# Sixteen transfers within HBM, given out behind the attention's gated products instead of at set planner times

## The chip, the cores and the metric

The kernel runs on one core of one Trainium2 chip. The metric is the device time of one execution in microseconds, as the median of several runs. Engine names in the profile: PE is TensorE (matmuls; PEld its weight loads), DVE is VectorE, ACT is ScalarE, POOL is GpSimd, SP is SyncE, which here only issues DMAs.

## The reference

One decoder block over 512 tokens of width 1024, in fp32:

```python
h = rms_norm(x, norm_pre)
proj = h @ w_in                       # q_n, six k/v of the attention, gates, z_n, q_r, k_r, v_r, z_r, m_a, m_b
o_a = nsa(...)                        # compressed, selected and sliding branch, gated and summed, per head
y_a = (o_a * silu(z_n)) @ w_nsa_o
o_b = retention(...)                  # four heads, chunks of 128, a running state, group norm
y_b = (o_b * silu(z_r)) @ w_ret_o
merged = sigmoid(m_a) * y_a + sigmoid(m_b) * y_b
y = x + rms_norm(merged @ w_out, norm_post)
```

The product `o_a * silu(z_n)` is what is called the gated product here.

## The kernel before

Every fp32 matrix product is made of three matmuls of rounded parts: high times high, high times low, low times high. The weights lie in one stream in HBM, in the order of use, in blocks of 128 rows by 1024 columns (512 KB). SyncE loads a block into one of four `raw` buffers (`NR`, line 28); a splitter then rounds each half to its high part `whi` (ScalarE or VectorE) and takes the rest `wlo` (VectorE, line 209). The next load into that buffer goes out when both halves are split (`load_next`, lines 347 to 369).

The order of work by products: the six keys and values, the gates, the queries, two hidden products of the compressed keys and values, and then `PLAN` (line 30): the gate Z, the merge gate MA of the first half, the retention's ZR, QK and VR twice over, with MB, NO and RO, and the second half. The attention's heads are worked between these products, token tile 3 first and 0 last. The last products are those with `w_out`.

Two of the products of the plan, the second halves of MA and MB (`SEVEN`, line 32), are done in Strassen's manner: seven products of half blocks instead of eight. This needs sums of quarter blocks of the weights. They are made in HBM, by DMAs that GpSimd issues, before the loads of those products read them as `raw<-t`. Per product there are four scratch tensors `t1` to `t4` (512 KB each) and eight transfers: four copies (t1 = b11, t3 = b12, t2 = b11, t4 = b21) and four that accumulate (t1 += b12, t3 += b22, t2 += t3, t4 += t2). With two products that makes 16, which go in turn for the one and the other (`weight_sums`, lines 327 to 337). An accumulation onto t2 needs the sums in t3, and one onto t4 needs t2.

The instructions are given out by a planner, `Order` (lines 45 to 118): each piece of work is a generator, which yields a planner time (or a condition, or a time with an engine) before it gives out instructions. The planner takes the pieces in the order of rank and of readiness, and keeps a clock per engine from fixed costs. The order in which it gives out an engine's instructions is the order of that engine's queue on the chip; the planner's times themselves are no part of the program. `weight_sums` yields 110000 ns plus 12000 ns for each further transfer (`T0`, `TSTEP`, line 41), and books 900 ns on the planner's GpSimd clock for each (line 337).

What else stands in GpSimd's queue: at the start memsets and masks, a power for the first norm (`rs`), four sums of the attention's gates with their bias (`gate`, in `tail_c`, line 622), then eight powers of the retention's group norm (`rv`, line 1082 in `ret`) and four powers of the last norm (`rr`, line 1336).

`ret` (line 1008) waits for the flags of all eight `att` sums before it goes on to its power. The flags are set in `att_sum` (line 920), one call for each of four token tiles and two groups. It adds the halves of a PSUM bank and multiplies with the gate:

```python
yield e, "pool"
gv = szn[m, :, t * P:(t + 1) * P]
e = tt(gv, low[m].rearrange("p (j c) -> p j c", j=4), gv, OP.mult, e)
NAT.put(low, e)
od.flags.add(f"att{t}{g}")
```

The helper is `def tt(o, a, b, op, r=0.0, e="dve")` (line 208): the fifth argument is the planner time from which the operands are there, the sixth the engine.

Of the kernel before, what the change touches and what calls it, by code (L numbers as in the profile page):

```python
# [37 lines left out]
SLACK = 700.0  # L38
WAKE = 7
HOLD = 1500.0  # L40
T0, TSTEP = 110000.0, 12000.0
DVE_BIAS = 400


# [95 lines left out]
def block_kernel(ctx: ExitStack, tc, x, xT, x0s, ws, small, w2s, norm_post, rope_r, dmask, out):  # L140
# [19 lines left out]
    def at(kb, n, dt=FT):  # L160
        o = int(kb * 256)
        if dt == FR:
            return arena_r[:, o:o + n]
        assert o >= 28 * 256 or o + n <= 28 * 256
        return arena_f[:, o - 28 * 256:o - 28 * 256 + n] if o >= 28 * 256 else arena_l[:, o:o + n]
# [30 lines left out]
    def act(o, i, func=AF.Copy, r=0.0, **kw):  # L196
        S.activation(o, i, func, **kw)  # L197
        return od.op("act", act_ns(o, i, lazy(kw.get("bias"), kw.get("scale"))) + (95 if "accum_out" in kw else 0), r)
# [9 lines left out]
    def tt(o, a, b, op, r=0.0, e="dve"):  # L208
        (V if e == "dve" else G).tensor_tensor(o, a, b, op=op)  # L209
        if op == OP.pow:  # L210
            return od.op(e, 300 + 164 * size(o), r, True)
        return od.op(e, (1.042 * size(o) + 69) if e == "dve" else (2.36 * size(o) + 77), r, e == "pool" or near(o, a, b))
# [98 lines left out]


    loads, off = [], 0
    sums = []
    for pieces in stream_shape():
        if pieces == "seven":
            b11, b12, b21, b22 = (ws[off + i * P * 1024:off + (i + 1) * P * 1024].rearrange("(p n) -> p n", p=P)
# [9 lines left out]
    def weight_sums():  # L327

        for n in range(8):
            for i, block in enumerate(sums):  # L330
                yield T0 + TSTEP * (n * len(sums) + i)
                o, a = block[n]
                if n < 4:
                    G.dma_start(o, a)
                else:
                    G.dma_start(o, a, accum_op=OP.add)
                od.op("pool", 900.0)
# [574 lines left out]
    def att_out():  # L912
        for t, g in ((t, g) for t in reversed(range(NT)) for g in range(2)):
            yield lambda: (t, g) in avs
            a = avs[t, g]
            po = yield from PO.get()
            a["po"] = po
            od.spawn(att_sum(t, g, po), 1)

    def att_sum(t, g, po):  # L920
        a = avs[t, g]
        yield lambda: a["n"] == a["total"]
        yield od.need("Z0", "Z1", "Z2", "Z3")
        m, o = slice(g * 64, g * 64 + 64), slice(64 - g * 64, 128 - g * 64)
        low = yield from NAT.get()
        yield a["e"], "act"
        e = act(low[m], po[o], r=a["e"])
        yield e, "dve"
        e = tt(low[m], po[m], low[m], OP.add, e)
        PO.put(po, e)  # L930
        yield e, "pool"
        gv = szn[m, :, t * P:(t + 1) * P]
        e = tt(gv, low[m].rearrange("p (j c) -> p j c", j=4), gv, OP.mult, e)
        NAT.put(low, e)
        od.flags.add(f"att{t}{g}")
        if all(n in od.flags for n in ATT):
            DMA.dma_start(dm, dmask.rearrange("h p c -> p h c"))
            dmr.append(od.dma(P * 2048, a["e"]))
            for o in (32, 36):
                VR[0].put((at(o, 512, FR), at(o + 2, 512, FR)))  # L940
            for _ in range(2):
                b = yield from PO.get()
                PS.put(b)
# [530 lines left out]
    od.spawn(splitter(), lambda: rank(nxt[0])())  # L1474
    od.spawn(edges(), 1)
    od.spawn(weight_sums(), 1)
    od.spawn(main(), MAIN)
    od.run()
# [28 lines left out]
def stream_shape():  # L1507

    yield [512, 512]
    yield from [[1024]] * 3  # L1510
    yield from [[560]] * 4
    yield from [[1024]] * (4 + 8)
    for b in PLAN:
        yield from ["seven"] if b in SEVEN else [[1024]] * (2 if b[0] == "NO" else 4)
    yield from [[1024]] * 8
# [67 lines left out]
```

## Time and profile before

| | us |
|---|---|
| median of 3 runs | 528.15 (527.85 to 531.55) |
| the profiled execution | 528.24 |
| its span in the trace | 526.5 |
| mean granted clock of TensorE in it | 0.997 of full speed |

The profile's rows give start and duration in us, engine, line of the kernel, operation, output and inputs by tile name, the count, and in brackets the idle time ahead with the engine that ended it. `t` is the scratch of the weight sums, `raw` the buffer of a weight load, `whi` and `wlo` its two parts, `bank` a PSUM bank; `arena_l`, `arena_f` and `arena_r` are large buffers shared by many tiles (`szn`, the gate, lies in `arena_l`), `nat` a small ring. "issue" ahead of an instruction is time in which its engine waited for nothing that the profile shows. DMA queue q0 is GpSimd's, q1 that of SyncE.

### The profile page before, as it was taken

To read this page: it belongs to the slowest core of one execution; us is meant where nothing else is said; L and a number is where in the kernel's file an instruction comes from. 1 tells how busy PE (TensorE), PEld (TensorE's weight loads), DVE (VectorE), ACT (ScalarE), POOL (GpSimd) and SP (SyncE) were. 2 spreads that over 40 slices of the span, in tenths; PEclk is the share of its full clock that TensorE was granted. 3 is DMA by queue.
4 is the path that set the end of the run, shared out by engine and by line. 5 is a ranking of instruction groups with operands and counts; after the bars stand their busy time and mean duration, and the time that the engine had idled before them with its cause. 6 is when DMAs were issued, how large, how long until landed. Compare 5 with 4: busy or idle time off the path is not lost.

```text
span 526.5 us, 7843 instructions
## 1 busy us (share of the span) xinstructions
PE 514.9 (98%) x2778; PEld 440.8 (84%) x2778; DVE 405.6 (77%) x980; ACT 290.5 (55%) x627; POOL 23.8 (5%) x48
## 2 busy tenths in 40 slices
PE   8989999999999999999999999999999999999995
PEld 7888888788888888888878888888788989988884
DVE  6698799989979889997886576786889867645533
ACT  6663798768557886784525353524557434323411
POOL 1002100000000000000111000000000000000000
PEclk9999999999999999999999999999999999999998
DMA  8956769601304004133543532141643726625032
GB/s 311 365 198 200 220 132 260 209 2 40 121 1 129 33 0 156 36 112 119 109 136 66 190 125 76 41 120 42 219 141 122 237 83 202 205 114 159 1 109 92
DMA packets 22456, 68.87 MB, mean 131 GB/s; under 512 B 2448, under 2 KB 3728, under 8 KB 22416
## 3 DMA queue, kind: packets, MB, share of 16 engines
q1 hardware_dynamic: 19968, 59.84, 33.9%
q0 software_dynamic: 2304, 8.39, 7.2%
q8 instruction: 22, 0.36, 0.3%
q10 hardware_dynamic: 144, 0.14, 0.1%
q14 instruction: 18, 0.15, 0.1%
HBM read 66.26 MB, written 10.49 MB: 146 GB/s over the span
## 4 chain that ended last, share of the span: by engine, by line
PE 81%; DVE 7%; DMA 7%; issue 2%; ACT 1%; SPq 1%; POOLq 0%; DVEq 0%; POOL 0%; ACTq 0%
PE bank L230 76%; DMA raw<-in_stream_dram 6%; PE bank L234 6%; DVE wlo L209 3%; DVE arena_r L209 1%; DMA arena_f<-in_xT_dram 1%; DVE arena_l L844 1%; DVE arena_f L209 1%; DVE arena_l L218 1%; ACT whi L197 0%; DVE nat L209 0%; ACT arena_l L197 0%; DVE whi L205 0%; SPq L477 0%; DVE arena_f L222 0%
## 5 line engine op out<-in xcount | busy, mean ns | idle before, releaser
L197 ACT ACTIVATE whi<-raw 128x512 fp32r<-128x512 f32 x159 | 95.7, 626 | 41.3 <-PE bank L230 32.2
L209 DVE TENSOR_TENSOR wlo<-raw,whi 128x512 fp32r<-128x512 f32 x172 | 111.7, 685 | 7.6 <-ACT whi L197 6.8
L230 PE MATMUL bank<-whi,hTh 128*128 128x512 f32 x256 | 99.7, 405 | 0.8 <-DVE arena_r L222 0.4
L230 PE MATMUL bank<-whi,hTl 128*128 128x512 f32 x256 | 96.2, 391 | 0.0
L230 PE MATMUL bank<-wlo,hTh 128*128 128x512 f32 x256 | 96.1, 391 | 0.0
L230 PE MATMUL bank<-arena_r 128*128 128x256 f32 (+2 forms) x328 | 70.7, 336 | 0.3 <-DVE arena_r L209 0.3
L230 PE MATMUL bank<-arena_r,whi 128*128 128x512 f32 (+1 forms) x208 | 63.8, 382 | 0.7 <-DVE sg L222 0.7
L197 ACT ACTIVATE arena_r<-bank 128x512 fp32r<-128x512 f32 (+2 forms) x80 | 45.2, 570 | 29.1 <-PE bank L234 27.7
L197 ACT ACTIVATE arena_l<-arena_l,stat 128x128 f32<-128x128 f32 (+3 forms) x104 | 55.3, 552 | 5.6 <-DVE stat L209 2.7
L209 DVE TENSOR_TENSOR arena_r<-bank,arena_r 128x512 fp32r<-128x512 f32 (+2 forms) x72 | 46.8, 656 | 13.8 <-ACT arena_r L197 13.1
L230 PEld LDWEIGHTS bank<-whi,hTl 128*128 128x128 f32 x256 | 48.0, 188 | 10.6
L230 PEld LDWEIGHTS bank<-arena_r 128*128 128x128 f32 x328 | 51.0, 189 | 6.5 <-DVE arena_r L209 0.6
L230 PEld LDWEIGHTS bank<-whi,hTh 128*128 128x128 f32 x256 | 48.0, 188 | 9.5 <-DVE arena_r L222 0.9
L230 PEld LDWEIGHTS bank<-wlo,hTh 128*128 128x128 f32 x256 | 48.3, 189 | 8.2
L230 PE MATMUL bank<-hTh,whi 128*128 128x512 f32 (+1 forms) x144 | 52.4, 364 | 0.0
L230 PE MATMUL bank<-hTh,wlo 128*128 128x512 f32 (+1 forms) x144 | 51.2, 355 | 0.0
L230 PE MATMUL bank<-hTl,whi 128*128 128x512 f32 (+1 forms) x144 | 51.1, 355 | 0.0
L230 PE MATMUL bank<-whi,arena_r 128*128 128x512 f32 (+1 forms) x176 | 48.7, 352 | 0.0
L230 PEld LDWEIGHTS bank<-arena_r,whi 128*128 128x128 f32 x208 | 38.8, 188 | 8.6 <-DVE sg L222 1.3
L230 PE MATMUL bank<-arena_r,wlo 128*128 128x512 f32 x96 | 37.4, 389 | 0.0
L230 PEld LDWEIGHTS bank<-whi,arena_r 128*128 128x128 f32 x176 | 32.1, 189 | 4.6
L230 PE MATMUL bank<-wlo,arena_r 128*128 128x512 f32 (+1 forms) x104 | 34.7, 343 | 0.3 <-DVE wlo L209 0.3
(164 smaller groups left out, 768.4 us busy)
## 6 DMA issues: line engine op xcount, KB each, us to landing
raw<-in_stream_dram SPq DMA_DIRECT2D x77, 512.0 KB, 4.3
t<-in_stream_dram POOLq DMA_DIRECT2D x12, 512.0 KB, 5.3
raw<-t SPq DMA_DIRECT2D x8, 512.0 KB, 3.7
arena_f<-in_rope_r_dram SPq DMA_DIRECT2D x8, 256.0 KB, 2.7
t<-t POOLq DMA_DIRECT2D x4, 512.0 KB, 5.4
arena_f<-in_xT_dram SPq DMA_DIRECT2D x8, 256.0 KB, 3.7
ends<-in_x_dram SPq DMA_DIRECT2D x4, 512.0 KB, 5.5
arena_l<-in_xT_dram SPq DMA_DIRECT2D x7, 256.0 KB, 5.7
```

The costliest lines, as they stand in the source:

```text
L197: S.activation(o, i, func, **kw)
L209: (V if e == "dve" else G).tensor_tensor(o, a, b, op=op)
L218: V.tensor_scalar(o, a, s1, s2, op0=op0, op1=op1)
L230: T.matmul(ps, a, b, start=start, stop=stop)
L234: T.transpose(ps, a, idn)
L844: V.tensor_tensor_reduce(pv[:, b, :], sv[:, b, :], maskp[:, 512 - L:512], 1.0, -NEG, OP.add, OP.min, nm[:, b:b + 1])
```

## The change

The 16 transfers are no longer given out at planner times, but by a count of the gated products given out so far: transfer number m (from 0) goes out when 2 x count exceeds m. The count rises by one in `att_sum`, next to the flag. The transfers, their order among themselves, and what they read and write stay.

```diff
-T0, TSTEP = 110000.0, 12000.0
+PER = 2
...
-    sums = []
+    sums, atts = [], [0]
...
         for n in range(8):
             for i, block in enumerate(sums):
-                yield T0 + TSTEP * (n * len(sums) + i)
+                while (n * len(sums) + i) >= PER * atts[0]:
+                    yield lambda: (n * len(sums) + i) < PER * atts[0]
                 o, a = block[n]
                 if n < 4:
                     G.dma_start(o, a)
...
         e = tt(gv, low[m].rearrange("p (j c) -> p j c", j=4), gv, OP.mult, e)
         NAT.put(low, e)
         od.flags.add(f"att{t}{g}")
+        atts[0] += 1
         if all(n in od.flags for n in ATT):
```

## The prediction

> **What bounds the kernel now.** I read the page first, for the engine that sets the end and for the transfers' share, and then the chain that ended last.
>
> ```profile
> PE 514.9 (98%) x2778; PEld 440.8 (84%) x2778; DVE 405.6 (77%) x980; ACT 290.5 (55%) x627; POOL 23.8 (5%) x48
> q1 hardware_dynamic: 19968, 59.84, 33.9%
> q0 software_dynamic: 2304, 8.39, 7.2%
> PE 81%; DVE 7%; DMA 7%; issue 2%; ACT 1%; SPq 1%; POOLq 0%; DVEq 0%; POOL 0%; ACTq 0%
> ```
>
> TensorE is busy 98% of the span, so a change pays or costs only where TensorE stands still. GpSimd is 5% busy; the 16 transfers are all that its queue q0 carries. Next is GpSimd's timeline, because the change moves instructions in that queue: start, duration, operation, and in brackets what the engine was idle for.
>
> ```profile
> 43.41 0.26 POOL L209 TENSOR_TENSOR gate<-nat,cst 128x24 f32<-128x24 f32 x1 [3.29 <-ACT nat L197]
> 43.62 1.78 POOL L334 DMA_DIRECT2D t<-in_stream_dram  x3
> ...
> 59.83 0.85 POOL L336 DMA_DIRECT2D t<-in_stream_dram  x1 [3.45 <-issue]
> 65.41 0.84 POOL L336 DMA_DIRECT2D t<-in_stream_dram  x1 [4.73 <-issue]
> 73.98 0.81 POOL L336 DMA_DIRECT2D t<-in_stream_dram  x1 [7.74 <-issue]
> 79.59 0.83 POOL L336 DMA_DIRECT2D t<-in_stream_dram  x1 [4.80 <-issue]
> 249.37 0.72 POOL L209 TENSOR_TENSOR rv<-rv,nhalf 128x2 f32<-128x2 f32 x1 [168.95 <-DVE rv L216]
> 250.07 0.86 POOL L336 DMA_DIRECT2D t<-t  x1
> 258.64 0.71 POOL L209 TENSOR_TENSOR rv<-rv,nhalf 128x2 f32<-128x2 f32 x1 [7.71 <-DVE rv L216]
> ...
> 285.56 0.87 POOL L336 DMA_DIRECT2D t<-t  x1
> ```
>
> This is the most important view. The planner's times for the 16 transfers start at 110 us (T0) and go up by 12 us, yet the first one runs at 43.62 us, straight behind the last gate sum. The planner's time only fixes a place in the queue; GpSimd goes on as soon as the instruction ahead is done. Twelve transfers (eight copies, four accumulations from the stream) follow the gate sum at once. The other four, t onto t, each stand behind one rv power of the retention and therefore run at 250 to 286 us.
>
> Where are the gated products? The instructions grouped by line, operation and shape, and the ones that write the same tile with their first and last start, say it.
>
> ```profile
> L209 DVE TENSOR_TENSOR arena_l<-nat,arena_l 64x512 f32<-64x512 f32 x8 | 5.5, 683 | 0.1
> L209 DVE TENSOR_TENSOR arena_l<-nat,arena_l x8: 676/684/691, 140.1 to 243.3; 64x512 f32<-64x512 f32 x8
> ```
>
> They are eight instructions of VectorE (DVE), not of GpSimd, between 140.1 and 243.3 us. The line names no engine, and the helper's default is VectorE. GpSimd's timeline has nothing between the last transfer of its first dozen and the power at 249.37.
>
> **The change part by part.** *What moves.* All 16 transfers are now given out while the eight products are, so before the first rv power, which waits for all eight products. In GpSimd's own queue that puts 16 instead of 12 behind the gate sum, with nothing between them. The first twelve keep their order and their time. The four t onto t, with their four DMAs, move from 250 to 286 us to straight behind 79.59. No transfer gets a wait on VectorE: it neither reads nor writes what a product does. The planner's only other trace of the transfers is 0.9 us each on its GpSimd clock, which stands far behind the work in both versions until the first power, so I take the other queues' orders as unchanged; a shift after 250 us I bound at 0.3 us either way, half of one 0.68 us product.
>
> *When the 13th runs.* Four rows of the transfers' landing, issued at 65.41, 73.98, 79.59 and, alone, 250.07:
>
> ```profile
> t<-in_stream_dram POOLq DMA_DIRECT2D x1, 512.0 KB, 8.3
> t<-in_stream_dram POOLq DMA_DIRECT2D x1, 512.0 KB, 5.3
> t<-in_stream_dram POOLq DMA_DIRECT2D x1, 512.0 KB, 8.2
> t<-t POOLq DMA_DIRECT2D x1, 512.0 KB, 5.2
> ```
>
> 65.41 + 8.3 = 73.71 and the next issue came at 73.98; 73.98 + 5.3 = 79.28 and the next came at 79.59. So an accumulation goes out 0.3 us after the one before has landed. The 13th goes out at 79.59 + 8.2 + 0.3 = 88.1 us. The 13th sums what the 11th (73.98) left, which has landed by then, so that adds no wait. The 14th follows at about 96.6 if the 13th takes 8.2, the 15th near 105, the 16th near 110. Behind them on GpSimd stands the first rv power, due at 249: nobody waits.
>
> *What is under way at 88.1.* The chain that ended last, in order of time:
>
> ```profile
> 81.82 7.29 DMA raw<-in_stream_dram
> ...
> 91.20 4.29 DMA raw<-in_stream_dram
> ...
> 98.39 1.64 PE bank L230 x8
> ```
>
> Here, and at few other places, the end hangs on loads of weights. The load issued at 81.82 met the 12th transfer (79.59 to 87.8) and took 7.29 us; the one issued at 91.20 met none and took 4.29. That second load carries the last weights of the gate product Z's first pass. From its landing at 91.20 + 4.29 = 95.5 the chain goes with no pause through the split to TensorE at 98.39. After that it stays on TensorE until 262.66, so what is lost at 98 is lost at the end.
>
> *Cost.* The 13th stands over the loads issued between 87.33 and 91.20. The nearest row is the load of 81.82 under the 12th: 7.29 - 4.29 = **3.0 us**, and I take it. Upper bound: against the shortest load, the one at 122.93 with nothing else moving (3.2 us, below), 7.29 - 3.2 = 4.1. Lower bound: the two queues take turns, 1.4 us, worked out as a rival below. No gain is possible here, for no transfer leaves this stretch. What is late next: the loads for the product MA, issued from 93.52 on, over which the 14th stands; their next use lets a buffer go only at 122.93, so they have some 20 us of cover, but for the first of them (a rival below). The 15th and 16th, 105 to 116 us, meet no load:
>
> ```profile
> raw<-in_stream_dram SPq DMA_DIRECT2D x1, 512.0 KB, 3.2
> 87.33 0.33 SPq L354 DMA_DIRECT2D raw<-in_stream_dram  x1
> 91.20 0.33 SPq L354 DMA_DIRECT2D raw<-in_stream_dram  x1
> 93.52 0.33 SPq L354 DMA_DIRECT2D raw<-in_stream_dram  x1
> 122.93 0.33 SPq L354 DMA_DIRECT2D raw<-in_stream_dram  x1
> 87.00:99.00 12.00, 11.56 (x65) 9.47 (x64) 10.48 (x21) 8.31 (x18) 0.00 (x0) 1.00 0.85 284
> 251.00:256.00 5.00, 5.00 (x29) 4.24 (x28) 3.54 (x8) 1.65 (x4) 0.00 (x0) 1.00 0.61 108
> ```
>
> The last two rows are stretches: length, then the busy time of PE, weight loads, VectorE, ScalarE, GpSimd, then clock, DMA share, GB/s. The DMA engines are 85% busy from 87 to 99, and one accumulation alone keeps them busy for 0.61 x 5 = 3.05 us.
>
> *Gain.* Taking the four away from 250 to 286 frees four issues of 0.87 us on GpSimd, behind which the next power comes over 8 us later: nothing. It frees the DMA engines there as well. TensorE's only wait on record between 248 and 300, and the chain ahead of it:
>
> ```profile
> PE bank L230 <- DVE arena_r L222: 0.4, 1, 0.4
> 262.68 0.43 DVE whi L205
> 263.11 2.40 DVE wlo L209 x4
> ```
>
> It is 0.4 us, behind a VectorE that works without a gap. Bounds 0 and 0.4; I take 0.2.
>
> *Sum.* The profiled execution took 528.24 us with its span of 526.5; the runs' median is 528.15, so the one stands for the other. 528.24 + 3.0 - 0.2 = **531.0 us**, half a per cent slower: within the 1% (5.3 us) that a measurement here can tell from no change.
>
> **The rivals.** *Turns instead of a standstill: 529.4.* If loads and accumulation share each engine packet by packet, a load is only slowed. One of q1's packets takes 0.339 x 526.5 x 16 / 19968 = 0.143 us; a transfer has 2304/16 = 144 packets. Each followed by one load packet, the 13th lasts 3.05 + 144 x 0.143/16 = 4.3 us, in which 144 load packets pass. Loads come every 1.9 us (two steps from 87.33 to 91.20), so 2.2 of them would have passed, each of some 175 packets (512 KB at 59.84 MB/19968 = 3.0 KB), or 391 packets. Missing 247 packets are 2.2 us of 16 engines; the idle 15% between 90 and 95.5 takes back 0.8: 1.4 us of stall. For it: q1 does move at 85% there when the 13th arrives, while the load of 81.82 came to engines already taken. Against: 7.29. [...]
>
> *Two hits: 533.8.* ScalarE takes its work in order:
>
> ```profile
> 98.08 0.63 ACT L197 ACTIVATE whi<-raw 128x512 fp32r<-128x512 f32 x1 [1.35 <-DMA raw<-in_stream_dram]
> 99.09 0.22 ACT L197 ACTIVATE kc<-bank 128x64 fp32r<-128x64 f32 x1 [0.38 <-PE bank L230]
> ```
>
> It already waits for the load issued at 93.52, MA's first, with the compressed keys (kc) behind it. If that load slips past 98 into the 14th, it is held twice: 3.0 + 3.0, less ScalarE's 0.38 of slack, is 5.6 us. Against: with the 13th's 4.3 us of traffic over by 94, that load should land before the 14th moves bytes.
>
> *Hidden anyway: 528.0.* Loads queued ahead go first and the 13th slips behind 95.5, leaving only the 0.2 gain. For it: loads are in the queue. Against: the same was so at 81.82.
>
> *The other side, the words hold: 525.2.* If GpSimd really paused for the products, all 16 would run between 140 and 244 us, and the load of 81.82 would take 4.29 instead of 7.29: 3.0 us gained, from the point at which the 12th lies behind 87. Against: 43.62 for a transfer planned at 110 us, and products on VectorE. That is also the case in which my reading of the edit is false: the changed kernel then does what its words say.
>
> **How the numbers follow.** The forecast 0.50, with its own range 529.4 (turns) to 532.3 (4.1 less 0.0); turns 0.15; hidden 0.15; two hits 0.13; the words hold 0.05; something not seen 0.02. Range 527.7 to 533.5: hidden less 0.3 (the runs' median less their lowest) at the foot, two hits less the 0.3 of the orders at the top. Slower by over 1% is above 533.4: most of two hits, 0.11. Faster by over 1%, below 522.9, has no case: 0.02. The rest, 0.87, is within 1%.
>
> **What would show it.** In GpSimd's timeline: 16 transfers from 43.6 on, the 13th at 88 and the 16th by 116, none at 250 to 286. In the chain: the load of 91.20 at 6 to 8 us instead of 4.29, and a TensorE wait of 2 to 4 us before 99. The products still on VectorE, and their first start near 143 instead of 140.1. Wrong I am if transfers appear between 140 and 244, if the load of 91.20 keeps its 4.3, or if the loss at 98 is there but gone by the end.

## The result, and the profile after

The changed kernel takes **532.31 us** as the median of 22 runs (529.55 to 534.89), the kernel before 528.81 us of 22 beside them (527.49 to 531.55). The ratio is **1.0062**, with a 95% interval of 1.0048 to 1.0077: 0.62% of 528.81 is 3.3 us lost (the two medians lie 3.5 us apart). The forecast was 531.0, 2.8 us over its own base. The profiled execution after took 529.98 us with a span of 528.1, near the lower end of its runs, so it shows less of the loss than the median does. Of the 22 runs the eight with a mean granted clock of TensorE of 0.994 or less took 532.2 to 534.7 us, the other 14 took 529.6 to 534.9 with a median of 531.5.

Its page, the lines that answer to those of before:

```profile
PE 516.8 (98%) x2778; PEld 440.7 (83%) x2778; DVE 405.7 (77%) x980; ACT 290.1 (55%) x627; POOL 24.0 (5%) x48
...
arena_f<-in_rope_r_dram SPq DMA_DIRECT2D x8, 256.0 KB, 2.7
t<-t POOLq DMA_DIRECT2D x4, 512.0 KB, 7.6
```

Instructions and bytes are those of before (4 + 12 transfers, 2304 packets in q0); what differs is that the four transfers t onto t now take a median of 7.6 us from issue to landing, where it was 5.4 before. GpSimd's timeline after:

```profile
43.27 0.24 POOL L209 TENSOR_TENSOR gate<-nat,cst 128x24 f32<-128x24 f32 x1 [2.91 <-ACT nat L197]
43.46 1.79 POOL L335 DMA_DIRECT2D t<-in_stream_dram  x3
...
66.48 0.84 POOL L337 DMA_DIRECT2D t<-in_stream_dram  x1 [4.93 <-issue]
72.22 0.81 POOL L337 DMA_DIRECT2D t<-in_stream_dram  x1 [4.90 <-issue]
77.95 0.83 POOL L337 DMA_DIRECT2D t<-in_stream_dram  x1 [4.93 <-issue]
83.59 0.82 POOL L337 DMA_DIRECT2D t<-t  x1 [4.81 <-issue]
90.90 0.83 POOL L337 DMA_DIRECT2D t<-t  x1 [6.49 <-issue]
99.64 0.82 POOL L337 DMA_DIRECT2D t<-t  x1 [7.91 <-issue]
108.07 0.82 POOL L337 DMA_DIRECT2D t<-t  x1 [7.61 <-issue]
251.46 0.72 POOL L209 TENSOR_TENSOR rv<-rv,nhalf 128x2 f32<-128x2 f32 x1 [142.57 <-DVE rv L216]
```

All 16 follow the gate sum at 43.46, and none stands in the stretch of the products, which are still VectorE's, from 142.2 us on:

```profile
L209 DVE TENSOR_TENSOR arena_l<-nat,arena_l x8: 675/683/691, 142.2 to 245.4; 64x512 f32<-64x512 f32 x8
```

So the change does not do what its words say. "Behind the products" holds only in the order in which the planner gives instructions out; GpSimd's own queue has no instruction there that waits for a product. The chain after, in order of time:

```profile
92.65 7.52 DMA raw<-in_stream_dram
...
100.25 0.64 ACT whi L197
...
102.86 0.44 PE bank L234 x2
```

The last load on it before a long stretch of TensorE is now that of 92.65, the first one for MA, whose counterpart before went out at 93.52. It was issued 1.75 us after the 14th transfer and took 7.52 us, where its counterpart took 4.5. The order of the instructions on TensorE, VectorE, ScalarE and SyncE is the same in both kernels, so one can follow the same matmul in both traces. Before and after, from TensorE's timeline, four that can be matched:

```profile
91.45 0.28 PE L230 MATMUL bank<-whi,arena_r 128*128 128x256 f32 x1
...
93.99 0.40 PE L230 MATMUL bank<-hTh,whi 128*128 128x512 f32 x1
...
97.44 0.39 PE L230 MATMUL bank<-hTh,whi 128*128 128x512 f32 x1
...
100.80 0.38 PE L234 MATMUL bank<-ident,arena_f 128*128 128x128 f32 x2
```

```profile
91.00 0.28 PE L230 MATMUL bank<-whi,arena_r 128*128 128x256 f32 x1
...
93.98 0.50 PE L230 MATMUL bank<-hTh,whi 128*128 128x512 f32 x1 [0.30 <-ACT whi L197]
...
98.85 0.40 PE L230 MATMUL bank<-hTh,whi 128*128 128x512 f32 x1
...
102.86 0.44 PE L234 MATMUL bank<-ident,arena_f 128*128 128x128 f32 x2 [0.39 <-DVE arena_r L209]
```

0.45 us early at 91.00, 0.01 early at 93.98, 1.41 late at 98.85, 2.06 late at 102.86: 2.5 us lost in 12. There is no one long wait, the longest is 0.39 us: TensorE takes each half block as it comes (from 93 to 103 us its weight loads waited three times for `whi`, 1.5 us in all, and three times for `wlo`, 1.3). The 2.06 us stay until 378 us, where 0.4 is given back.

### The profile page after: what moved, and what is told of

Read it like the earlier page. It is cut to its first block, busy times and chain, and to the rows that moved or that the text cites. A ratio compares the mean times of both kernels' runs of the same rounds, so it can differ in the third digit from the quotient of the medians.

```text
span 528.1 us, 7843 instructions
## 1 busy us (share of the span) xinstructions
PE 516.8 (98%) x2778; PEld 440.7 (83%) x2778; DVE 405.7 (77%) x980; ACT 290.1 (55%) x627; POOL 24.0 (5%) x48
## 3 DMA queue, kind: packets, MB, share of 16 engines
q0 software_dynamic: 2304, 8.39, 7.1%
## 4 chain that ended last, share of the span: by engine, by line
PE 80%; DVE 7%; DMA 7%; issue 2%; ACT 2%; SPq 0%; POOLq 0%; DVEq 0%; POOL 0%; ACTq 0%
PE bank L230 75%; DMA raw<-in_stream_dram 6%; PE bank L234 6%; DVE wlo L209 3%; DVE arena_r L209 1%; DMA arena_f<-in_xT_dram 1%; ACT arena_l L197 1%; DVE arena_f L209 1%; DVE arena_l L218 1%; ACT whi L197 0%; DVE nat L209 0%; DVE arena_l L845 0%; ACT arena_f L197 0%; DVE whi L205 0%; DVE arena_l L209 0%
## 5 line engine op out<-in xcount | busy, mean ns | idle before, releaser
L234 PE MATMUL bank<-ident,arena_l 128*128 128x128 f32 (+1 forms) x232 | 34.0, 273 | 0.9 <-DVE arena_l L565 0.9
```

The costliest lines, as they stand in the source:

```text
L234: T.transpose(ps, a, idn)
```

## The experiments

Nine kernels were run, each in five rounds beside the kernel before; ratios are to that kernel. In all of them the instruction orders of TensorE, VectorE, ScalarE and SyncE are those of before. My theory: the loss comes from the bytes of the 13th transfer, which now runs over the loads of Z's first pass. Rivals: the waits or issues in GpSimd's queue, the other three transfers, or a price by turns.

**The last four left out** (edit of the changed kernel).

```diff
-                else:
+                elif n < 6:
                     G.dma_start(o, a, accum_op=OP.add)
```

> The changed kernel without the four transfers t onto t (their sums are missing in the weights read later). Theory A (the loss is those transfers' traffic over the weight loads issued between 87 and 98 us): back to the kernel before or a shade under, ratio 0.998 to 1.001, and no step of delay on TensorE between 94 and 101 us. Rival B (the loss has to do with something else that the new place of the transfers brings, an order or a wait): stays at 1.005 to 1.007.

Measured: 528.58, ratio 1.0003 [0.9987, 1.0019]. The whole loss goes with the four. Nothing of it comes from the way in which the first twelve are given out.

**The last four cut to 16 of 1024 columns**, which keeps the four issues and takes the bytes away.

```diff
+                elif n < 6:
+                    G.dma_start(o, a, accum_op=OP.add)
                 else:
-                    G.dma_start(o, a, accum_op=OP.add)
+                    G.dma_start(o[:, 0:16], a[:, 0:16], accum_op=OP.add)
```

> The changed kernel with the four transfers t onto t cut to 16 of 1024 columns (the rest of those sums is missing): GpSimd's four instructions and their places stay, the bytes go down to 1/64. Theory A (the DMA engines' time is what costs): 0.998 to 1.002. Rival C (what costs is GpSimd's issuing, 0.8 us each, next to a busy VectorE, or the waits in its queue): 1.004 to 1.007.

Measured: 528.69, ratio 0.9995 [0.998, 1.001]. Four issues in GpSimd's queue at the same place cost nothing; the bytes do.

**Only the 13th early** (edit of the kernel before: the 13th gets the planner time of the 12th, the other three stay behind their powers).

```diff
-                yield T0 + TSTEP * (n * len(sums) + i)
+                k = n * len(sums) + i
+                yield T0 + TSTEP * (11 if k == 12 else k)
```

> The kernel before with the 13th transfer alone moved to straight behind the 12th; the other three stay behind the rv powers. Theory A as predicted (one hit, by the 13th): nearly the whole loss is there, ratio 1.004 to 1.007. Rival D (two hits: the 14th holds up the loads as well): about half, 1.002 to 1.004. Rival B: 1.000.

Measured: 532.29 (528.5 to 535.1), ratio 1.006 [1.0034, 1.0086]. The 13th alone costs what the whole change costs; the 14th to 16th add nothing that the intervals can show. The profiled execution, at 533.22, is one of the long ones and shows the stall at its clearest. GpSimd's timeline, the chain and TensorE's timeline:

```profile
86.39 0.82 POOL L337 DMA_DIRECT2D t<-t  x1 [6.05 <-issue]
```

```profile
87.88 8.30 DMA raw<-in_stream_dram
```

```profile
93.42 0.39 PE L230 MATMUL bank<-hTh,wlo 128*128 128x512 f32 x1
96.95 0.64 PE L230 MATMUL bank<-hTh,whi 128*128 128x512 f32 x1 [3.14 <-ACT whi L197]
```

The load issued 1.5 us behind the transfer takes 8.30 us, and TensorE stands for 3.14. Its counterpart before is the load of 87.33, landed after 4.6. How the two queues share the engines is in the rows of the DMA queues (packets, MB, share of the 16 engines). From 88 to 92 us, of this run and then of the kernel before, which has no accumulation there:

```profile
q0 software_dynamic: 127, 0.46, 66.2%
q1 hardware_dynamic: 76, 0.30, 22.0%
```

```profile
q1 hardware_dynamic: 309, 1.12, 84.1%
```

From 87 to 89 us of the changed kernel, while its own 13th moves:

```profile
q0 software_dynamic: 90, 0.37, 93.3%
q1 hardware_dynamic: 33, 0.08, 11.8%
```

In both, the accumulation has the engines nearly to itself for 2 us and most of its 144 packets: 90 of them here at a share of 93.3%, beside 33 of the loads, and 93 in the run with only the 13th early, from 89 to 91 us at 102.2%, beside one of the loads (last section).

**Really behind the products** (edit of the changed kernel: a GpSimd copy that reads the product stands ahead of each pair). This tests the rival "the words hold".

```diff
+    tok = sp.tile([P, 1], FT, name="tok")
...
         e = tt(gv, low[m].rearrange("p (j c) -> p j c", j=4), gv, OP.mult, e)
+        G.tensor_copy(tok[m], gv[:, 0, 0:1])
```

> The changed kernel with one small GpSimd copy of a column of each gated product ahead of its two transfers, so that GpSimd's queue really waits for VectorE's product. The transfers should run between 142 and 255 us. Theory A (a transfer over loads that the chain hangs on costs; elsewhere it costs nothing): faster than before, 525 to 526.5, ratio 0.993 to 0.996, since the load of 81.82 too is free of the 12th. Rival E (the first twelve cost nothing where they are, since TensorE waits little there): as before, 0.999 to 1.001. Rival F (the DMA engines meet loads again between 142 and 255 us, or the first rv power waits behind the last transfers): 1.002 or more.

Measured: 541.44, ratio 1.0241 [1.0217, 1.0264]: far slower, where the rival had 525.2 and my theory 525 to 526.5. GpSimd's timeline and the chain:

```profile
141.16 0.70 POOL L936 COPY tok<-arena_l 64x1 f32<-64x1 f32 x1 [96.58 <-DVE arena_l L209]
...
228.46 0.83 POOL L338 DMA_DIRECT2D t<-in_stream_dram  x1 [4.89 <-issue]
...
261.27 0.82 POOL L338 DMA_DIRECT2D t<-t  x1 [4.65 <-issue]
262.16 0.73 POOL L209 TENSOR_TENSOR rv<-rv,nhalf 128x2 f32<-128x2 f32 x1
```

```profile
229.86 7.35 DMA arena_f<-in_rope_r_dram
...
265.51 1.12 PE bank L234 x4
```

Two things went wrong there. The 12th transfer, at 228.46, held a load of the rotary table for 7.35 us, where the median of those is 2.7. And the first power of the retention stands behind the last transfers in the queue: it ran at 262.16 instead of 249.37, and TensorE waited 7.5 us for what follows from it. Followed matmul by matmul against the kernel before, TensorE in this profile is 0.3 us late at 98.73, 4.1 at 243.71 and 14.4 at 271.12: about 3.7 us came in the stretch of the table, 10.3 in that of the power.

**The last four behind the gate Z** (the first twelve as before; a GpSimd copy of a column of Z's first finished tile ahead of the 13th).

```diff
-                while (n * len(sums) + i) >= PER * atts[0]:
-                    yield lambda: (n * len(sums) + i) < PER * atts[0]
+                if n < 6:
+                    yield 60000.0
+                while n >= 6 and not atts[0]:
+                    yield lambda: atts[0] > 0
...
+        if j == 0:
+            G.tensor_copy(tok, szn[:, 0, 0:1])
+            atts[0] = 8
...
-        atts[0] += 1
```

> As the changed kernel, but ahead of the 13th transfer stands a GpSimd copy of one column of Z's first tile, which VectorE finishes at about 102 us; the first twelve stay where they were. The same four transfers move by some 15 us, to 102 to 126 us, where at most the one load of 123 us meets them. Theory A (the place over the loads of 87 to 93 us is the whole cost): 0.999 to 1.001. Rival G (four accumulations ahead of the rv powers cost wherever they stand, by the DMA engines or by memory): 1.003 to 1.007.

Measured: 527.96, ratio 0.9998 [0.9979, 1.0016]. GpSimd's timeline:

```profile
102.00 0.18 POOL L654 COPY tok<-arena_l 128x1 f32<-128x1 f32 x1 [21.81 <-DVE arena_l L222]
...
102.57 0.82 POOL L340 DMA_DIRECT2D t<-t  x1 [0.40 <-issue]
```

The same four transfers, still some 147 us earlier than before, cost nothing once the 13th starts at 102.57. So the price lies in the stretch ahead of that, where the loads of Z's first pass and of MA's start are under way.

**No transfers at all**: the loads read plain quarter blocks in place of the sums, so the two products of Strassen's manner are computed from other data.

```diff
-            loads.extend((a, [1024]) for a in (b11, b21, t2, t3, t1, t4, b22))
+            loads.extend((a, [1024]) for a in (b11, b21, b11, b12, b11, b21, b22))
...
-                if n < 4:
-                    G.dma_start(o, a)
-                else:
-                    G.dma_start(o, a, accum_op=OP.add)
-                od.op("pool", 900.0)
+                pass
```

> The changed kernel without any of the 16 transfers; the loads that read sums read plain weight blocks instead (the sums are missing). It bounds what can be gained by a better place. My prediction's account of the load of 81.82 (held for 3.0 us by the 12th, on the chain): 0.993 to 0.996. What the run with the transfers behind the products showed up to 98 us (that load took 3.5 and TensorE was no earlier): 0.998 to 1.000, for behind that load VectorE is the next limit.

Measured: 526.64 (526.38 to 527.63), ratio 0.9969 [0.9954, 0.9984]. That is 1.6 us, and a bound on what any place of the 16 can gain. It lies between the two ranges that were expected, and the interval reaches into both. The chain shows what takes the loads' place when no transfer holds them: VectorE until 78.86, and from there on TensorE itself, past 104 us.

```profile
78.25 0.61 DVE arena_r L209
...
78.91 0.50 PE bank L230
```

**All 16 behind the first product**, with one copy on GpSimd (`PER = 16`), so that they are through long before the first power.

```diff
-PER = 2
+PER = 16
...
         e = tt(gv, low[m].rearrange("p (j c) -> p j c", j=4), gv, OP.mult, e)
+        if not atts[0]:
+            G.tensor_copy(tok[m], gv[:, 0, 0:1])
```

> All 16 transfers behind a GpSimd copy of a column of the first product only: they should run from 141 to about 205 us, clear of the loads of 87 to 98, of the load at 229 and of the first rv power at 249. Theory A: no loss, 0.998 to 1.000, thus as good as without transfers and a little better than before. Rival H (the loads between 141 and 205 us have as little cover): 1.003 or more.

Measured: **527.24** (526.58 to 528.19), ratio 0.9976 [0.9964, 0.9988]: better than both kernels by more than the interval, near the bound above. GpSimd's timeline, and the stretch of the transfers (length, then the busy times of PE and the others, the clock, the DMA share, GB/s):

```profile
140.61 0.70 POOL L937 COPY tok<-arena_l 64x1 f32<-64x1 f32 x1 [96.57 <-DVE arena_l L209]
141.26 1.80 POOL L336 DMA_DIRECT2D t<-in_stream_dram  x3
...
198.01 0.82 POOL L338 DMA_DIRECT2D t<-t  x1 [4.66 <-issue]
249.18 0.73 POOL L209 TENSOR_TENSOR rv<-rv,nhalf 128x2 f32<-128x2 f32 x1 [50.35 <-DVE rv L216]
```

```profile
140.00:204.00 64.00, 64.00 (x340) 54.14 (x339) 55.90 (x163) 48.89 (x116) 11.78 (x17) 1.00 0.70 173
```

In 64 us with all 16 transfers TensorE does not stand still once, and the power runs at 249.18, as before.

**One more transfer ahead of the 13th** (edit of the changed kernel; it adds 512 KB to a scratch that nobody reads).

```diff
+    spare = dp.tile([P, 1040], FT, name="spare")[:, 0:1024]
...
+                if n * len(sums) + i == 12:
+                    G.dma_start(spare, sums[0][4][0], accum_op=OP.add)
```

> The changed kernel with one more accumulation of 512 KB, into a spare tensor, between the 12th and the 13th. Theory A with one hit: the extra one takes the 13th's place, the 13th the 14th's, so little is added, 1.006 to 1.008. Rival D (each transfer over the stretch adds its own 3 us): 1.010 to 1.013.

Measured: 531.9, ratio 1.0073 [1.0052, 1.0093]: not to be told from the change itself. Its profile, of a run at 534.32, has two held loads in the chain, those of 84.53 and 94.80, of 8.20 and 7.84 us, so this execution was hit twice.

**Four behind each product** (the copies of the slower kernel above, with `PER = 4`).

```diff
-PER = 2
+PER = 4
...
+        G.tensor_copy(tok[m], gv[:, 0, 0:1])
```

> As the run with two transfers behind each product and GpSimd really waiting, but with four behind each, so that the last four follow the fourth product at 189 us and end by about 212. If that run lost its 2.4% because its last transfers stood ahead of the first rv power and its 11th and 12th over the loads of 229 us, both are gone here: 0.996 to 0.999, like all 16 behind the first product. If instead the wait for the products, or the small copies, cost by themselves: 1.005 or more.

Measured: 527.8 (526.14 to 529.53), ratio 0.9979 [0.9958, 1.0001]. The eight copies and their waits cost nothing that shows. So the loss at two behind each came from where the late transfers lay: next to the table's load and ahead of the first power.

## Why the prediction was right, and where it was not

**What bounds the kernel, and what moves: right.** The planner's times place an instruction in a queue and do not hold it (a transfer planned at 110 us ran at 43.62); the products are VectorE's; the twelve follow the gate sum; the four t onto t follow them; nothing else changes its place in any queue. Without the last four the loss is gone, and a copy that reads the product did make GpSimd wait (the first one ran at 141.16, behind 96.58 us of idle time).

**When the 13th runs: too late by 1.7 to 4.5 us.** I took 8.3, 5.3 and 8.2 us for the landing of the 10th to 12th from one trace. After, they were issued 5.7, 5.7 and 5.6 us apart (66.48, 72.22, 77.95, 83.59), and the 13th came at 83.59; with only the 13th early it came at 86.39. The "0.3 us after the landing" held (83.59 + 7.0 = 90.59 and the next came at 90.90; 99.64 + 8.1 = 107.74 and the next came at 108.07), but the landings differ from one profile to the next (the 10th took 8.3 us before and 5.4 after). So my chain of sums had a spread of its own that I did not give it. The 14th came at 90.90 (96.6 expected) and the 15th at 99.64 (105 expected), where it lay over three of MA's loads, which landed by 103.97; they had cover, and TensorE's 2.06 us did not grow. The 16th, at 108.07, met no load, as forecast.

**Which load is held: only half right.** The counterpart of the load of 91.20 went out at 90.33 in the changed kernel and landed after 6.7 us, inside the 6 to 8 expected, but not for the reason given:

```profile
raw<-in_stream_dram SPq DMA_DIRECT2D x1, 512.0 KB, 6.7
```

The 13th, issued at 83.59, landed after 7.0 us, at 90.59, so it was the 14th that lay over this load. The 13th lay over the loads of 87.14 and 89.12. And the load that ended on the chain was MA's first, held by the 14th, which is the mechanism of the rival "two hits", for which my ground against was a 14th at 96.6. Its price was wrong: TensorE went from 0.45 us early to 1.41 late over the two transfers, and MA's load brought it to 2.06, not to 5.6. How much of the 1.41 is the 13th's and how much the 14th's the trace does not part. The one TensorE wait of 2 to 4 us that I named as a sign is not there either. With only the 13th early it was the load two before that of 91.20, and there the long wait came. The stretch and the mechanism were right; the one load was not mine to name from one trace.

**The cost: 3.0 forecast, 3.3 measured in all.** That they lie so close is in part luck. In the changed kernel's profile TensorE lost 2.5 us in the stretch, by two transfers and not by one. With only the 13th early it waited 3.14 us, and on top came a granted clock of 0.50 that I had not foreseen (last section): from 0.33 us early to 4.56 late, 4.9 us in all. The range of 1.4 to 4.1 around the term holds the first two and not the last. The 3.3 stands over executions with and without the lower clock. The 1% that I took as the least a measurement can tell was too coarse: the interval here is 0.3% wide.

**The gain of 0.2: did not come.** The four transfers left 250 to 286 us, and TensorE's wait there is as long as before, once 0.4 us for `arena_r` of line 222. VectorE stands in front of it, not the DMA engines. The lower bound, 0, was the answer; "No gain is possible here", said of the stretch at 88, was right.

**Turns, 529.4: not what the time shows.** That is 1.2 us over the base; the interval of the ratio is 2.5 to 4.1 us. In the run with only the 13th early the loads moved 76 packets in 4 us at a share of 22.0%, while the transfer took 66.2%. One load packet behind each packet of the transfer, from which this sum and the 1.4 us at the foot of the cost's range are worked out, was my assumption, and no run shows it: in that run 93 packets of the transfer stood beside one of the loads from 89 to 91 us. *Hidden anyway, 528.0*, is excluded by the interval. (The sums of two other rivals left out the gain of 0.2 that this one and turns take: with it, two hits is 533.6 and the words hold 525.0.)

**The words hold, 525.2: wrong in sign.** That rival priced the load of 81.82 under the 12th at 3.0 us, because it stood on the chain. With all 16 gone the gain is 1.6 us, and with all of them at 141 to 204 it is 0.24%, or 1.3 us. A load on the chain that ended last is worth only the distance to the next thing that is late, and with no transfers that is TensorE's own work from 78.91 on. I also had put nothing behind the last pair: the first power shares their queue and came 12.8 us later (262.16 against 249.37), of which some 4 us were lost before, in the stretch of the table. The price of a moved transfer is read in the place where it lands and from everything queued behind it.

**What stays open.** The changed kernel and the one with only the 13th early scatter over 5.3 and 6.6 us; with no transfers, or with all behind the first product, it is 1.3 and 1.6 us. That points to the transfers next to the loads of 44 to 105 us, which the kernel before has as well (4.1 us). But with four behind each product none lies there, and it is still 3.4 us, so the cause of the scatter is not shown. How a run's timing of the 10th to 12th decides which load is held, and so its time, was seen in single profiles only and not settled.

## What to carry to other kernels

A planner's time or a condition in the generator ordered the queue here and delayed nothing: a transfer planned at 110 us ran at 43.62, and one planned behind the products at 43.46. What held a DMA back was an instruction ahead of it on its engine that reads what it is to wait for (the copy at 141.16), and then everything behind it in that queue waited as well (the power at 262.16 instead of 249.37). The transfers within HBM were free where TensorE ran without a pause for the whole of them and no power or load was due behind them (140 to 204 us, ratio 0.9976), and dear where loads were only just in time (83 to 104 us, 1.0062). Price a held load against the next late thing, not against its own length, and give a chain of issue times worked out from one trace a range.

## What the runs showed of the hardware that was not expected

**A stop of TensorE cost more than its length.** With only the 13th early TensorE stood 3.14 us, and then ran at a granted clock of 0.50. Three stretches of 1 us of that run (the clock is the third number from the end):

```profile
96.00:97.00 1.00, 0.05 (x1) 0.05 (x1) 0.07 (x1) 0.73 (x2) 0.00 (x0) 1.00 0.54 221
...
98.00:99.00 1.00, 1.00 (x4) 0.81 (x3) 0.30 (x2) 1.00 (x3) 0.00 (x0) 0.50 0.07 29
...
101.00:102.00 1.00, 1.00 (x6) 0.82 (x5) 1.00 (x3) 0.00 (x0) 0.00 (x0) 1.00 0.83 127
```

The 0.50 lasted from about 97 to 100.5. The matmul that follows the wait runs 2.96 us later than its counterpart before, and eight matmuls on, at 100.40, it is 4.56: those eight steps took 3.45 us, where they took 1.85 before, so the slow clock added 1.6 us. At 105.24, where the counterpart stands at 100.80, 4.44 are left. The changed kernel's profiled run, whose longest wait here was 0.39 us, kept 1.00. In the kernel with two really behind each product a shorter wait, the one of 1.90 us that ended at 240.21, behind the table's load, was followed by 0.50 as well. One of 1.86 us that ended at 32.92 in the same run was not:

```profile
32.92 0.41 PE L234 MATMUL bank<-ident,arena_f 128*128 128x128 f32 x2 [1.86 <-DVE arena_f L566]
...
240.21 0.64 PE L230 MATMUL bank<-wlo,hTh 128*128 128x512 f32 x1 [1.90 <-DVE wlo L209]
```

```profile
33.00:37.00 4.00, 3.10 (x24) 2.88 (x25) 3.65 (x23) 3.20 (x12) 0.54 (x2) 1.00 0.49 158
...
241.00:243.00 2.00, 2.00 (x6) 1.15 (x5) 2.00 (x5) 0.42 (x1) 2.00 (x1) 0.50 0.98 346
```

So the clock was 0.50 for about 3.5 us behind the wait of 3.14 us, and two waits of nearly the same length, 1.86 and 1.90 us, had different outcomes: the length alone did not decide here. What did is not shown.

**An accumulation within HBM brought the loads almost to rest.** In the rows of 88 to 92 us of the run with only the 13th early (with the experiment), the loads had 76 packets and 22.0% of the engines in 4 us; before, with no accumulation there, they had 309 and 84.1%. In the middle of it, from 89 to 91 us, they had one packet (a packet counts where it starts, so a share can pass 100%):

```profile
q0 software_dynamic: 93, 0.37, 102.2%
q1 hardware_dynamic: 1, 0.00, 0.5%
```

From the rows of 88 to 92, one packet of the accumulation held an engine for 0.662 x 4 x 16 / 127 = 0.33 us, one of the loads 0.220 x 4 x 16 / 76 = 0.19, and before 0.841 x 4 x 16 / 309 = 0.17. So the loads' packets were hardly slower than before, which speaks against the memory as the bottleneck; there were few of them. The accumulation's 144 packets are 144 x 0.33 / 16 = 3.0 us of every engine, the size that the forecast took from the load of 81.82. Why the loads did not get every second turn is not in the traces.
